# A hybrid attention trunk on one core: a rewritten opening, VectorE a chunk ahead, and two pieces of work moved behind others

## The chip, the core and the metric

One core of a Trainium2 chip runs the whole program. The core has five engines with their own instruction queues: TensorE (PE; its weight loads are shown as PEld), VectorE (DVE), ScalarE (ACT), GpSimd (POOL) and SyncE (SP), which here only issues transfers. The metric is the device time of one launch in microseconds (us), the median over several runs; smaller is better.

## What is computed

Two layers over a sequence of 512 positions of width 1024 (`x`, kept transposed: 8 chunks of 128 features by 512 positions). Each layer normalises `x`, modulates it by a conditioning vector `c`, and multiplies the result `h` by one wide input matrix; two attention mixers (8 heads each) work on the parts, and an output matrix closes the layer.

```
c_act = silu(c)
for l in range(2):
    shift, scale, gate = split(c_act @ w_ada[l] + b_ada[l], 3)
    h = rms_norm(x, norm_g[l]) * (1 + scale) + shift
    fq, fk, fv, ff, fg, q_lat, kv_lat, k_r, mg = split(h @ w_in[l])
    y_fox = fox_attention(fq, fk, fv, log_sigmoid(ff + b_f[l])) * silu(fg)
    q = rms_norm(q_lat, q_norm_g[l]) @ w_uq[l];  q_rope = rope(q, cos, sin)
    kv = rms_norm(kv_lat, kv_norm_g[l]) @ w_ukv[l];  k_rope = rope(k_r, cos, sin)
    y_mla = mla_attention(q, q_rope, kv, k_rope) * silu(mg)
    x = x + gate * (concat(y_fox, y_mla) @ w_out[l])
return rms_norm(x, final_g)
```

Every large product of float32 numbers is made of three products of rounded operands: high by high, high by low, low by high, where the low part is what the rounding left (`mm3`, L238 to L241). So each weight tile and each chunk of `h` needs a cast on ScalarE (`hi_of`, L124) and a subtraction on VectorE (`lo_of`, L127).

## The kernel before

**The opening** is `start_first` (L417 to L507). SyncE loads `c`, spread over 128 partitions (512 KB, L145), then a 512 KB tile of the modulation matrix (`ada`), then the 8 chunks of `x` (256 KB each, L465), then `ada` and weights (`w_first`) in turns. ScalarE and VectorE make `cb`, twice the silu of `c` on all partitions. TensorE warms up on 20 dummy products (L473). ScalarE squares each chunk of `x` and TensorE adds the squares over partitions by a float32 product with ones (L477); `Ln` and `Exp` on ScalarE give `r`, the reciprocal root (L478, L479).

**The chunk loop** then takes the 8 chunks of features one after the other. For chunk k VectorE sums two `ada` tiles along the free axis (`along`, L271) into the scalars A and B (L457, L258), multiplies `x` by A and `r` (L385), ScalarE adds B and casts (`hh`, L388), VectorE makes the rest (`hl`, L389); the weights of the chunk are cast and split as above (L124, L127, a piece of 512 columns and one of 304). TensorE then runs 21 products for the chunk: three for a 48-column tile called small (the forget gates and the rotary key), three for the first key tile, three for the first query tile, and twelve for the four tiles of `v`. The eight chunks add into seven banks of PSUM. The angles for the rotary embedding (`trig`) are computed in the loop, between the chunks' own work.

**Behind the chunk loop** `mix` runs six steps in order (`before`): the forget gates with the rotary key (`small`, L546), the first query and key (L655, L673), the first gate, and the query and key of the second pair of heads. The first gate and that query and key are projections of 24 products each, whose weights come through three buffers for the high and three for the low part. Then a loop over 64 units runs the scores and transposes of both mixers; between the units it takes work from a list (`fill_a`, `fill_b`), in the order of the table `ORD_A`.

**The order on each engine.** TensorE's order is the order of the code (`manual_schedule`). VectorE, ScalarE and the others are ordered by a scheduler at build time, and each engine then works strictly in that order. An instruction that waits therefore holds up all that stands behind it on its engine. Transfers are issued by SyncE, in order, and an issue can wait for a buffer or for an earlier transfer.

Of the kernel before, what the change touches and what calls it, by code (L numbers as in the profile page):

```python
# [52 lines left out]
WARM = 20  # L53
TRIG_AT = (2,2,3,5,6,)
FIRST_ORDER = (2,1,0,)
PRIO = 200
ORD_A = ((0,1,2,3,4,5,6,10,7,8,9,11,12,13,15,14,16,17,),(0,1,2,3,5,6,4,7,8,9,10,11,12,13,14,15,16,17,),)
# [11 lines left out]
PIN_ROWS = (0,2,3,)  # L69
PE_ENGINE = mybir.EngineType.PE  # L70
FIRST_W = 816
FIRST = ((512, P), (640, P), (768, 48))
# [12 lines left out]
def trunk(ctx, tc, xT_in, pos, c_in, cols_in, w_first, w_proj, w_small, w_v, w_uq, w_ukv, w_out, ada_0, ada_r, out):  # L85
# [39 lines left out]

    def lo_of(dst, src, hi, eng=None):
        (eng or nc.vector).tensor_sub(out=dst, in0=src, in1=hi.bitcast(F32))  # L127
# [15 lines left out]
    for half in range(2):  # L143
        cs = slice(512 * half, 512 * half + 512)
        nc.sync.dma_start(out=cb[:, cs], in_=c_in[:, cs].broadcast_to([P, 512]))  # L145
        th = scr()
        nc.scalar.activation(out=th, in_=cb[:, cs], func=AF.Tanh, scale=0.5)
        nc.vector.scalar_tensor_tensor(out=cb[:, cs], in0=th, scalar=1.0, in1=cb[:, cs], op0=ALU.add, op1=ALU.mult)
# [38 lines left out]
    def trig():  # L187
# [5 lines left out]
        nc.vector.tensor_copy(out=ang, in_=pi)  # L193
        nc.vector.tensor_scalar(out=ang, in0=ang, scalar1=col(C_INV), scalar2=None, op0=ALU.mult)
        nc.vector.tensor_scalar(out=kk, in0=ang, scalar1=1.0 / TWO_PI, scalar2=ROUND_MAGIC,
                                op0=ALU.mult, op1=ALU.add)
        nc.vector.tensor_scalar(out=kk, in0=kk, scalar1=-ROUND_MAGIC, scalar2=None, op0=ALU.add)
        for part in (PI_A, PI_B, PI_C):
            nc.vector.scalar_tensor_tensor(out=ang, in0=kk, scalar=-part, in1=ang,
                                           op0=ALU.mult, op1=ALU.add)  # L200
        yield
        nc.scalar.activation(out=sin, in_=ang, func=AF.Sin)
        nc.scalar.activation(out=cos, in_=ang, func=AF.Sin, scale=0.5)
        yield
        nc.vector.tensor_mul(out=cos, in0=cos, in1=cos)
        nc.vector.tensor_scalar(out=cos, in0=cos, scalar1=-2.0, scalar2=1.0, op0=ALU.mult, op1=ALU.add)
# [21 lines left out]
    def parts_w(raw, n, eng=None):  # L228
        with prio(boost[0]):
            lo = wp.tile([P, 1024], F32R, tag="wl", bufs=W_BUFS, name=nm("wl"))  # L230
            hi = wp.tile([P, 1024], F32R, tag="wh", bufs=W_BUFS, name=nm("wh"))
            ins = hi_of(hi[:, :n], raw[:, :n])
            if hold[0] and "w" in PIN_S:
                behind(ins, hold[0], "after the forget gates")
            lo_of(lo[:, :n], raw[:, :n], hi[:, :n], eng)
# [33 lines left out]
    def along(raw, cs, dst):  # L269

        nc.vector.scalar_tensor_tensor(out=raw, in0=raw, scalar=0.5, in1=cb[:, cs], op0=ALU.mult, op1=ALU.mult,  # L271
                                       accum_out=dst)
# [95 lines left out]
    class Layer:  # L368
# [11 lines left out]
        def h_chunk(self, k, cs, x, r, lo_eng=None):  # L380
            l = self.l
            t = scr()
            b = B_c[l][:, k:k + 1]
            hh, hl = self.hh[k][:, cs], self.hl[k][:, cs]
            nc.vector.scalar_tensor_tensor(out=t[:, cs], in0=x[k][:, cs], scalar=A_c[l][:, k:k + 1], in1=r[:, cs],  # L385
                                           op0=ALU.mult, op1=ALU.mult)
            if lo_eng is None:
                nc.scalar.activation(out=hh, in_=t[:, cs], func=AF.Identity, bias=b)  # L388
                nc.vector.scalar_tensor_tensor(out=hl, in0=t[:, cs], scalar=b, in1=hh.bitcast(F32),  # L389
                                               op0=ALU.add, op1=ALU.subtract)  # L390
            else:
                nc.scalar.activation(out=t[:, cs], in_=t[:, cs], func=AF.Identity, bias=b)
                hi_of(hh, t[:, cs])
                lo_of(hl, t[:, cs], hh, lo_eng)
# [728 lines left out]
```

## Time and profile before

| | us |
|---|---|
| median of 3 runs | 581.97 |
| lowest, highest | 577.22, 582.1 |
| the profiled execution | 580.7 |
| its span, first to last instruction | 578.8 |
| TensorE busy in the span | 552.0 (95%) |
| VectorE busy | 435.2 (75%) |
| ScalarE busy | 369.7 (64%) |
| mean granted TensorE clock | 0.985 |

Times below count from the start of the span of the profiled execution. "Granted clock" is TensorE's clock as a share of full speed; in this profile it stands at 1.00 or at 0.50 (2.4 and 1.2 GHz). A 512-column product of rounded operands starts 0.23 us after the one before it at full clock and 0.43 us after it at half clock. An idle time in brackets at the end of a row is what the engine waited before that instruction, and for whom.

### The profile page before, as it was taken

The numbers are of one execution on the slowest core, as the hardware profiler recorded it, in microseconds if no ns is written. First come the engines' busy times: TensorE is split into PE (matmuls) and PEld (weight loads), VectorE is DVE, ScalarE is ACT, GpSimd is POOL, SyncE is SP. The second block draws the span as 40 slices with busy tenths as digits, with TensorE's granted clock in tenths as the row PEclk, the third lists the DMA queues.
The fourth block names the chain that finished last, engine by engine and source line by source line (L and its number), as shares of the span: only waits on it lengthen the run. The fifth ranks groups of instructions, "written<-read, shape, count | busy, mean of one in ns | idle before, by whom it ended". The sixth has DMA issues, their size and how long they took to land.

```text
span 578.8 us, 8543 instructions
## 1 busy us (share of the span) xinstructions
PE 552.0 (95%) x2932; PEld 438.7 (76%) x2932; DVE 435.2 (75%) x938; ACT 369.7 (64%) x787; POOL 32.7 (6%) x57
## 2 busy tenths in 40 slices
PE   8799989999899998999989999999999999999994
PEld 6477868777677676877988888877777767777893
DVE  2898777777758878969699486676597988964664
ACT  6343836766657878973377354667477777877642
POOL 4000020110001000000000030001001000000011
PEclk9799989999989999999999999999999999999998
DMA  8985134342313544769744324322133341441534
GB/s 283 404 315 168 51 114 147 112 147 74 112 47 79 170 130 129 226 236 303 249 142 145 110 78 147 110 75 75 56 110 87 93 116 46 134 128 36 170 104 145
DMA packets 36859, 81.08 MB, mean 140 GB/s; under 512 B 7616, under 2 KB 13760, under 8 KB 36816
## 3 DMA queue, kind: packets, MB, share of 16 engines
q1 hardware_dynamic: 35792, 80.28, 42.8%
q8 instruction: 23, 0.38, 0.3%
q0 software_dynamic: 1024, 0.27, 0.3%
q14 instruction: 20, 0.16, 0.1%
HBM read 72.36 MB, written 4.72 MB: 133 GB/s over the span
## 4 chain that ended last, share of the span: by engine, by line
PE 68%; DVE 13%; ACT 7%; DMA 7%; issue 3%; SPq 0%; POOL 0%; DVEq 0%; ACTq 0%; POOLq 0%
PE psp L239 13%; PE psp L241 13%; PE psp L240 13%; PE psa L625 5%; PE pst L613 4%; PE pss L239 3%; DMA scr<-mrow 3%; PE pss L241 3%; PE pss L240 3%; DVE wl L127 2%; DMA raw<-in_w_out 2%; PE pss L693 2%; ACT wh L124 1%; ACT p L601 1%; DVE st L599 1%
## 5 line engine op out<-in xcount | busy, mean ns | idle before, releaser
L239 PE MATMUL psp<-sl,wh 128*128 128x512 f32 (+1 forms) x488 | 188.7, 387 | 0.1
L241 PE MATMUL psp<-sl,wl 128*128 128x512 f32 (+1 forms) x488 | 179.7, 368 | 3.7 <-DVE wl L127 3.7
L240 PE MATMUL psp<-sl,wh 128*128 128x512 f32 (+1 forms) x488 | 178.9, 367 | 0.0
L241 PEld LDWEIGHTS psp<-sl,wl 128*128 128x128 f32 x488 | 92.9, 190 | 20.2 <-DVE wl L127 4.8
L239 PEld LDWEIGHTS psp<-sl,wh 128*128 128x128 f32 x488 | 93.5, 192 | 12.6 <-ACT vf L411 0.4
L240 PEld LDWEIGHTS psp<-sl,wh 128*128 128x128 f32 x488 | 93.6, 192 | 11.1 <-DVE sl L127 0.2
L127 DVE TENSOR_TENSOR wl<-raw,wh 128x1024 fp32r<-128x1024 f32 (+1 forms) x62 | 73.4, 1186 | 26.1 <-ACT wh L124 25.6
L601 ACT ACTIVATE p<-pss,st 128x128 f32<-128x128 f32 (+3 forms) x128 | 67.3, 527 | 25.8 <-DVE st L599 25.2
L124 ACT CAST wh<-raw 128x1024 fp32r<-128x1024 f32 (+1 forms) x63 | 63.5, 1013 | 30.0 <-DMA raw<-in_w_out 9.4
L604 ACT ACTIVATE p<-p,st 128x128 f32<-128x128 f32 (+3 forms) x128 | 70.9, 564 | 17.1 <-DVE st L602 16.7
L599 DVE TENSOR_REDUCE st<-pss 128x1 f32<-128x128 f32 (+3 forms) x128 | 61.8, 484 | 21.8 <-PE pss L695 14.9
L613 PE MATMUL pst<-ident,p 128*128 128x128 f32 x320 | 57.0, 276 | 0.2 <-ACT p L604 0.2
L619 ACT COPY pT<-pst 128x512 f32<-128x512 f32 (+2 forms) x72 | 31.6, 439 | 24.7 <-PE pst L613 24.0
L124 ACT CAST sl<-scr 112x512 fp32r<-112x512 f32 (+1 forms) x48 | 29.4, 616 | 19.5 <-DVE scr L631 15.4
L613 PEld LDWEIGHTS pst<-ident,p 128*128 128x128 f32 x320 | 37.9, 142 | 4.1 <-ACT p L604 0.8
L127 DVE TENSOR_TENSOR sl<-scr,sl 112x512 fp32r<-112x512 f32 (+1 forms) x48 | 32.7, 685 | 5.8 <-ACT sl L124 5.4
L602 DVE RECIPROCAL st<-st 128x1 f32<-128x1 f32 x128 | 19.7, 157 | 19.9 <-ACT p L601 19.1
L271 DVE SCALAR_TENSOR_TENSOR adr<-adr,cb 128x1024 f32<-128x1024 f32 x24 | 29.1, 1214 | 3.8 <-DMA adr<-in_ada_r 3.7
L639 POOL DMA_DIRECT2D sl<-csq x16 | 9.2, 574 | 327.6 <-issue 157.6
L239 PE MATMUL pss<-sl,sl 112*128 112x256 f32 (+2 forms) x64 | 23.0, 359 | 3.5 <-ACT p L601 3.2
L617 DVE COPY pT<-pst 128x384 f32<-128x384 f32 (+2 forms) x56 | 25.2, 451 | 0.4 <-PE pst L613 0.2
L388 ACT ACTIVATE sl<-scr,B 128x256 fp32r<-128x256 f32 (+1 forms) x24 | 12.8, 574 | 19.7 <-DVE scr L385 17.3
(195 smaller groups left out, 894.4 us busy)
## 6 DMA issues: line engine op xcount, KB each, us to landing
raw<-in_w_proj SPq DMA_DIRECT2D x36, 512.0 KB, 3.5
adr<-in_ada_r SPq DMA_DIRECT2D x24, 512.0 KB, 3.5
raw<-in_w_out SPq DMA_DIRECT2D x20, 512.0 KB, 4.3
sl<-in_w_v SPq DMA_DIRECT2D x16, 256.0 KB, 5.0
sl<-in_ada_r SPq DMA_DIRECT2D x16, 256.0 KB, 5.0
vm<-in_ada SPq DMA_DIRECT2D x6, 512.0 KB, 6.0
pT<-in_ada SPq DMA_DIRECT2D x6, 512.0 KB, 6.7
sl<-in_xT SPq DMA_DIRECT2D x8, 256.0 KB, 6.1
```

Source lines behind the costliest of these rows:

```text
L124: return nc.scalar.copy(out=dst, in_=src) if scale == 1.0 else nc.scalar.mul(out=dst, in_=src, mul=scale)
L127: (eng or nc.vector).tensor_sub(out=dst, in0=src, in1=hi.bitcast(F32))
L239: nc.tensor.matmul(out=ps, lhsT=lh, rhs=rh, start=first, stop=False)
L240: nc.tensor.matmul(out=ps, lhsT=lh, rhs=rl, start=False, stop=False)
L241: nc.tensor.matmul(out=ps, lhsT=ll, rhs=rh, start=False, stop=last)
L271: nc.vector.scalar_tensor_tensor(out=raw, in0=raw, scalar=0.5, in1=cb[:, cs], op0=ALU.mult, op1=ALU.mult, accum_out=dst)
L599: nc.vector.tensor_reduce(out=st[:, 0:1], in_=s[:, :w], op=ALU.max, axis=AX, negate=True)
L601: nc.scalar.activation(out=p[:, :w], in_=s[:, :w], func=AF.Exp, bias=st[:, 0:1], accum_out=st[:, 1:2])
L604: nc.scalar.mul(out=p[:, :w], in_=p[:, :w], mul=st[:, 2:3])
L613: nc.tensor.transpose(out=tp[:, j * P:(j + 1) * P], in_=p[:, j * P:(j + 1) * P], identity=ident)
L619: nc.scalar.copy(out=dst, in_=src)
L625: nc.tensor.matmul(out=ps[64 * a:64 * a + 64, j * P:T], lhsT=v[:, j, 64 * heads[a]:64 * heads[a] + 64], rhs=pTs[a][:, PT_J * j + P * j:PT_ ...
```

## The change

- **Opening.** `c` is loaded as one row of 4 KB and activated on one partition; two products with a row of ones spread it over the partitions, and ScalarE copies them to `cb`. The positions are loaded third, the first five chunks of `x` next, then the first `ada` tile and the rest of `x`. The angles are computed before the chunk loop. Chunks 1, 3 and 5 of `x` are squared on VectorE and added there to the square of the chunk before, so TensorE gets five products with squares and not eight. There are 12 dummy products at first, 5 after the spreading products, and 3 of 512 columns behind the last product with squares. The table of the logarithm is loaded between the squares of chunks 6 and 7, and none is loaded for the forget gates later.
- **Chunk loop.** VectorE's and ScalarE's orders are now pinned (`queue`), from strings of letters: m for a modulation step, h for a step of `h`, w for a step of the weights, capitals for the next chunk. The products of a chunk are ordered by turn: all seven tiles with high weights and `hh`, then with `hl`, then six with low weights. The small tile is 112 columns wide and carries its low weights beside the high ones, so it takes two products: 20 for a chunk.
- **Rotary key.** Its four VectorE instructions leave `small` and become a piece of fill (`key`, number 18 in `ORD_A`), behind the first latent projection, in both layers.
- **Second gate moved behind.** In the first layer's list, gate 8 now stands behind the third key 11 and the sums 9.

```diff
-WARM = 20
-TRIG_AT = (2,2,3,5,6,)
-ORD_A = ((0,1,2,3,4,5,6,10,7,8,9,11,12,13,15,14,16,17,),(0,1,2,3,5,6,4,7,8,...
+WARM, WARM_1, WARM_2 = 12, 5, 3
+SQ_V, CB_AT, ANGLES = (1, 3, 5), (2, 4), 2
+TRIG_AT = (3, 4)
+ORD_A = ((0,18,1,2,3,4,5,6,10,7,11,9,8,12,13,15,14,16,17,),(0,18,1,2,3,5,6,4,7,8,...
+LOGS_AT = 6
+FIRST_W, FIRST_S, FIRST = 832, 768, (512, 640)
...
+    def queue(engine, ins):
+        if engine in line:
+            if line[engine]:
+                behind(ins, line[engine], "order of the first chunks")
+            line[engine] = ins.ins.name
+        return ins
...
-        nc.sync.dma_start(out=cb[:, cs], in_=c_in[:, cs].broadcast_to([P, 512]))
+    nc.sync.dma_start(out=c_row[0:1, :], in_=c_in)
+    nc.scalar.activation(out=c_act[0:1, :], in_=c_row[0:1, :], func=AF.Tanh, scale=0.5)
...
             def split_first(k):
+                queue("a", hi_of(hi[:, 512:FIRST_W], b[:, :FIRST_W - 512]))
+                yield
+                queue("a", hi_of(hi[:, :512], a))
+                yield
+                queue("v", lo_of(lo[:, 512:FIRST_S], b[:, :FIRST_S - 512], hi[:, 512:FIRST_S]))
+                queue("v", lo_of(hi[:, FIRST_S + SM_H:FIRST_S + SM_ALL], b[:, FIRST_S - 512:FIRST_S - 512 + SM],
+                                 hi[:, FIRST_S:FIRST_S + SM]))
+                yield
+                queue("v", lo_of(lo[:, :512], a, hi[:, :512]))
+                yield
...
             for k in range(KC):
                 sq = scr()
-                nc.scalar.activation(out=sq, in_=x0[k], func=AF.Square)
-                nc.tensor.matmul(out=total, lhsT=ones, rhs=sq, start=k == 0, stop=k == KC - 1)
+                if k in SQ_V:
+                    queue("v", nc.vector.tensor_mul(out=sq, in0=x0[k], in1=x0[k]))
+                    queue("v", nc.vector.tensor_add(out=sq, in0=before, in1=sq))
+                else:
+                    queue("a", nc.scalar.activation(out=sq, in_=x0[k], func=AF.Square))
...
+                if k == LOGS_AT:
+                    queue("a", nc.scalar.preload_act_table_set("natural_log_exp_and_others"))
...
+            for _ in range(WARM_2):
+                nc.tensor.matmul(out=first[0], lhsT=ones, rhs=x0[0], start=True, stop=True)
+            make(0, "mmwwhhwhwWMHM")
...
+                    make(k + 1, "hwwMhwWHM")
...
+                for turn, (ws, hs) in enumerate(((hi, self.hh), (hi, self.hl), (lo, self.hh))):
...
+        def key(self):
+            yield 0.0
+            t = self.key_in
             u, v = scr(), scr()
             nc.vector.tensor_mul(out=u[:SM, :], in0=t[:SM, :], in1=cosT[:SM, :])
```

Three places in the built programs show what the prediction speaks of. **ScalarE at the end of the opening**, from the last squares (`scr<-sl`) through `Ln` and `Exp` (`aux`) and the casts of the first weights (`wh`) to the first chunk of `h`. Before:

```order
L476 ACTIVATE scr_230<-sl_87 128x512
L476 ACTIVATE scr_233<-sl_88 128x512
L478 ACTIVATE aux_167<-pst_163,eps_c 128x512
L124 CAST wh_246<-sl_180 128x512
L479 ACTIVATE aux_167<-aux_167 128x512
L124 CAST wh_246<-sl_181 128x304
L388 ACTIVATE sl_146<-scr_255,B_125 128x512
```

And now:

```order
L519 ACTIVATE scr_240<-sl_87 128x512
L530 ACT_TABLE_LOAD
L519 ACTIVATE scr_244<-sl_88 128x512
L532 ACTIVATE aux_247<-pst_160,eps_c 128x512
L533 ACTIVATE aux_247<-aux_247 128x512
L124 CAST wh_265<-sl_186 128x320
L124 CAST wh_265<-sl_185 128x512
L399 ACTIVATE sl_143<-scr_268,B_122 128x512
```

A table load now stands between the last two squares, and both casts stand between `Exp` and the first chunk of `h`.

**VectorE in one round of the chunk loop** (`sums` are the `along` sums, `A` and `B` the scalars, `scr` is `x` by A by `r`, `sl` with `B` is `hl`, `wl` the low weights). Before:

```order
L258 TENSOR_TENSOR B_125<-sums_168,cols 128x1
L385 SCALAR_TENSOR_TENSOR scr_277<-sl_82,A_123,aux_167 128x512
L271 SCALAR_TENSOR_TENSOR raw_259,sums_168<-raw_259,cb 128x1024
L389 SCALAR_TENSOR_TENSOR sl_155<-scr_277,B_125,sl_147 128x512
L457 TENSOR_SCALAR A_123<-sums_168,b_109,cols 128x1
L271 SCALAR_TENSOR_TENSOR raw_261,sums_168<-raw_261,cb 128x1024
L127 TENSOR_TENSOR wl_308<-sl_263,wh_309 128x512
L127 TENSOR_TENSOR wl_308<-sl_264,wh_309 128x304
```

And now:

```order
L477 TENSOR_TENSOR B_122<-sums_164,cols 128x1
L137 TENSOR_TENSOR wl_300<-sl_289,wh_301 128x256
L137 TENSOR_TENSOR wh_301<-sl_289,wh_301 128x48
L282 SCALAR_TENSOR_TENSOR vm_161,sums_164<-vm_161,cb 128x1024
L473 TENSOR_SCALAR A_120<-sums_164,b_106,cols 128x1
L401 SCALAR_TENSOR_TENSOR sl_153<-scr_303,B_122,sl_145 128x512
L137 TENSOR_TENSOR wl_300<-sl_288,wh_301 128x512
L396 SCALAR_TENSOR_TENSOR scr_344<-sl_84,A_120,aux_247 128x512
L282 SCALAR_TENSOR_TENSOR pT_162,sums_164<-pT_162,cb 128x1024
```

The same work stands in a round, with one instruction more (the 304 columns are now 256 and 48), and the next chunk's `along` and product with `x` stand between this chunk's steps.

**VectorE behind the chunk loop**, from the forget gates' scan (`scr` from two `scr`) on; `csk` and `csq` are its results, `wl` from `raw` the low weights of the projections, `mrow` the rotary key, `gate` the first gate. Before, behind the scan:

```order
L580 TENSOR_TENSOR scr_603<-lat_581,cosT 48x512
L576 CAST csk<-scr_592 32x512
L576 CAST csq<-scr_592 32x512
L577 TENSOR_TENSOR csk<-scr_592,csk 32x512
L577 TENSOR_TENSOR csq<-scr_592,csq 32x512
L581 TENSOR_TENSOR scr_604<-lat_581,sinT 48x512
L662 SCALAR_TENSOR_TENSOR sl_614<-psp_242,sl_614 64x512
L582 TENSOR_TENSOR mrow<-scr_603,scr_604 16x512
L583 TENSOR_TENSOR mrow<-scr_603,scr_604 16x512
L664 CAST sl_615<-sl_614 64x512
L590 SCALAR_TENSOR_TENSOR gate_672<-scr_670,psp_645 128x512
L127 TENSOR_TENSOR wl_676<-raw_674,wh_677 128x1024
```

And now, from the row of the same low weights on:

```order
L137 TENSOR_TENSOR wl_674<-raw_672,wh_675 128x1024
L631 SCALAR_TENSOR_TENSOR scr_596<-scr_594,scr_595 32x512
L726 SCALAR_TENSOR_TENSOR sl_612<-psp_254,sl_612 64x512
L635 CAST csk<-scr_596 32x512
L635 CAST csq<-scr_596 32x512
L636 TENSOR_TENSOR csk<-scr_596,csk 32x512
L636 TENSOR_TENSOR csq<-scr_596,csq 32x512
L728 CAST sl_613<-sl_612 64x512
L137 TENSOR_TENSOR wl_760<-raw_758,wh_761 128x1024
L654 SCALAR_TENSOR_TENSOR gate_670<-scr_668,psp_643 128x512
L644 TENSOR_TENSOR scr_823<-lat_584,cosT 48x512
```

The low weights of the third projection (the second pair's key) moved from behind the scan, the key and the gate to ahead of the scan, and the rotary key moved behind the gate.

## Rows read from the trace of the kernel before

**Rows 1.** Page, part 1: busy time of each engine and its share of the span.
```profile
PE 552.0 (95%) x2932; PEld 438.7 (76%) x2932; DVE 435.2 (75%) x938; ACT 369.7 (64%) x787; POOL 32.7 (6%) x57
```

**Rows 2.** Windows: stretch, length, busy time per engine (instructions), granted clock, DMA share, GB/s.
```profile
0.00:19.58 19.58, 13.87 (x56) 9.50 (x56) 7.46 (x18) 11.69 (x18) 6.05 (x17) 0.99 0.89 314
19.58:27.88 8.30, 7.52 (x22) 5.36 (x23) 8.30 (x18) 2.44 (x5) 0.00 (x0) 0.62 1.04 407
27.88:32.71 4.83, 4.83 (x22) 3.75 (x21) 4.83 (x11) 1.58 (x3) 0.00 (x0) 1.00 1.04 400
73.40:83.00 9.60, 6.85 (x23) 5.39 (x23) 7.37 (x10) 1.98 (x3) 2.95 (x6) 0.82 0.36 115
156.80:163.20 6.40, 4.42 (x21) 3.74 (x20) 5.50 (x11) 3.08 (x7) 0.00 (x0) 0.73 0.24 83
```

**Rows 3.** Chain that ended last, opening: start, us, engine or transfer and line.
```profile
2.20 0.43 SPq L439
2.67 5.64 DMA sl<-in_xT
8.34 0.64 ACT scr L476
9.02 7.15 PE pst L477 x16
```

**Rows 4.** Timeline, ScalarE in the opening: start, us, line, operation, [idle before].
```profile
7.02 1.28 ACT L462 ACT_TABLE_LOAD   x1
...
16.19 0.69 ACT L478 ACTIVATE aux<-pst,eps_c 128x512 f32<-128x512 f32 x1 [2.10 <-PE pst L477]
16.78 0.61 ACT L124 CAST wh<-sl 128x512 fp32r<-128x512 f32 x1
17.29 0.63 ACT L479 ACTIVATE aux<-aux 128x512 f32<-128x512 f32 x1
17.82 0.43 ACT L124 CAST wh<-sl 128x304 fp32r<-128x304 f32 x1
```

**Rows 5.** Page, part 6: transfers, count, KB each, median us from issue to landing.
```profile
sl<-in_xT SPq DMA_DIRECT2D x8, 256.0 KB, 6.1
...
cols<-in_cols SPq DMA_DIRECT2D x1, 40.5 KB, 1.9
```

**Rows 6.** Timeline, VectorE through one round of the chunk loop.
```profile
25.74 0.27 DVE L457 TENSOR_SCALAR A<-sums,b,cols 128x1 f32<-128x1 f32 x1
25.92 1.22 DVE L271 SCALAR_TENSOR_TENSOR raw<-raw,cb 128x1024 f32<-128x1024 f32 x1
...
27.07 1.07 DVE L127 TENSOR_TENSOR wl<-sl,wh 128x512 fp32r<-128x512 f32 x2
28.05 0.15 DVE L258 TENSOR_TENSOR B<-sums,cols 128x1 f32<-128x1 f32 x1
28.12 0.75 DVE L385 SCALAR_TENSOR_TENSOR scr<-sl,A,aux 128x512 f32<-128x512 f32 x1
...
30.59 0.27 DVE L457 TENSOR_SCALAR A<-sums,b,cols 128x1 f32<-128x1 f32 x1
```

**Rows 7.** Timeline behind the chunk loop, ScalarE, VectorE and TensorE.
```profile
59.91 1.27 ACT L411 COPY vf<-pss 128x512 f32<-128x512 f32 x2
...
61.91 0.50 PE L239 MATMUL psp<-sl,wh 128*128 128x512 f32 x1
...
67.09 1.21 DVE L572 TENSOR_TENSOR_SCAN scr<-scr,scr 32x512 f32<-32x512 f32 x1 [2.81 <-ACT scr L569]
...
76.31 0.51 PE L241 MATMUL psp<-sl,wl 128*128 128x512 f32 x1 [2.75 <-DVE wl L127]
```

**Rows 8.** Timelines, TensorE's first score of all and two later waits.
```profile
83.04 0.28 PE L693 MATMUL pss<-sl,sl 128*128 128x256 f32 x1
...
158.82 0.43 PE L693 MATMUL pss<-sl,sl 128*128 128x256 f32 x1 [1.98 <-DVE sl L682]
...
219.03 0.44 PE L239 MATMUL pss<-sl,sl 112*128 112x384 f32 x1 [1.58 <-ACT p L601]
```

More of the change, by code (lines that the diff above doesn't have):

```diff
@@ new lines, in modulate, with make @@
+                yield
+                queue("v", along(ada[0, k], ALL1, d[:, 0, s]))
+                queue("v", nc.vector.tensor_add(out=B_c[0][:, s], in0=d[:, 0, s], in1=cols[:, C_BA + k:C_BA + k + 1]))
+                yield
+            steps = {}
+            def make(k, order):
+                for i, c in ((k, "mhw"), (k + 1, "MHW")):
+                    for name, g in zip(c, (modulate, lambda k: self.h_chunk(k, ALL, x0, r), split_first)):
+                        if i < KC and (i, name.lower()) not in steps:
+                            steps[i, name.lower()] = g(i)
+                for c in order:
+                    i = k if c in "mhw" else k + 1
+                    if i < KC:
+                        next(steps[i, c.lower()])
@@ L464, in start_first @@
+            for _ in range(ANGLES):
+                next(angles)
             for k in range(KC):
                 nc.sync.dma_start(out=x0[k], in_=xT_in[:, k, :])
+                if k == 4:
+                    load_ada(1, 0)
             load_ada(0, 0)
@@ L470, in start_first @@
             load_first(1)
-            next(angles)
             for _ in range(WARM):
+                nc.tensor.matmul(out=total[:, 0:P], lhsT=ones, rhs=ones, start=True, stop=True)
+            spread_c = [bank("p") for _ in range(2)]
+            for half in range(2):
+                nc.tensor.matmul(out=spread_c[half], lhsT=ones[0:1, :], rhs=c_act[0:1, 512 * half:512 * half + 512],
+                                 start=True, stop=True)
+            for _ in range(WARM_1):
                 nc.tensor.matmul(out=total[:, 0:P], lhsT=ones, rhs=ones, start=True, stop=True)
@@ L496, in start_first @@
                 hi, lo = w[k]
[L497 to L501 removed]
+                for turn, (ws, hs) in enumerate(((hi, self.hh), (hi, self.hl), (lo, self.hh))):
+                    a, b = turn == 0 and k == 0, turn == 2 and k == KC - 1
+                    if turn < 2:
+                        nc.tensor.matmul(out=first[2][:SM_ALL, :], lhsT=hi[:, FIRST_S:FIRST_S + SM_ALL], rhs=hs[k],
+                                         start=a, stop=turn == 1 and k == KC - 1)
+                    for j in (1, 0):
+                        o = FIRST[j]
+                        nc.tensor.matmul(out=first[j], lhsT=ws[:, o:o + P], rhs=hs[k], start=a, stop=b)
+                    for ti, ps in vps.items():
+                        nc.tensor.matmul(out=ps, lhsT=hs[k][:, ti * P:(ti + 1) * P], rhs=ws[:, :512], start=a, stop=b)
             for _ in range(TRIG_AT.count(KC)):
@@ L1025, in enter_second @@
         for k in range(KC):
-            lay[1].h_chunk(k, cs, lay[0].x, r)
+            for _ in lay[1].h_chunk(k, cs, lay[0].x, r):
+                pass
         if half == 1:
```

116 lines of the change are left out of this document (53 added, 63 removed).

## Prediction

> **What bounds the kernel now.** I read the busy times first: TensorE is busy for 552.0 of 578.8 us [rows 1], so only places where it waits or runs slowly can give time. The windows by stage show them [rows 2]: it is fully busy at full clock in most stretches, but not before 19.58 (the opening), not in the first chunk (8.30 us where the next takes 4.83, granted clock 0.62), not at 73.40 to 83.00 (clock 0.82) and not at 156.80 to 163.20 (clock 0.73). Last I read what ended each wait. In the opening the chain runs through the loading of `x`, the squares and eight products of 0.89 us each [rows 3], then `Ln`, `Exp` and the casts on ScalarE [rows 4]. At 76.31 a projection had waited 2.75 us for low weights from VectorE, which had itself waited 2.81 us for ScalarE's logarithm ahead of the scan [rows 7]. At 158.82 a score had waited 1.98 us for the third key's low part [rows 8]. The change touches all four places. Behind them both kernels run the same TensorE work, so I carry a gain there to the end.
>
> **Start of the first chunk.** The fourth issue stood at 2.20 [rows 3]; `x` now takes that place. Between its issue and landing 1.9 us (41 KB) is the low bound and 6.1, `x`'s own median behind a megabyte of other loads, the high one [rows 5]. Only small loads stand ahead, so I take 3.5, nearer the low end: chunk 0 at 5.7 (bounds 4.1 and 8.3). Chunk 6 comes eight pieces of 256 KB later (six chunks and one `ada` tile), at 400 GB/s [rows 2] 0.66 us each: 11.0. Then, each behind the other on ScalarE [rows 3, 4]: square 0.64, table load 1.28, square of chunk 7 0.64, one product 0.89, `Ln` 0.69, `Exp` 0.63; with 0.1 between engines that is 15.9. Now both casts stand ahead of the first `hh`: 0.43 and 0.61; `hh` itself is like `Ln`, 0.7. The first product starts at 17.7 instead of 19.58: 1.9 us earlier (bounds 16.1 to 20.3, so a loss of 0.7 is possible). Spreading `c` by two products and two copies, the angles (ten VectorE instructions on 64 columns) and their table load fill time in which these engines now wait for `x`; uncovered, each table load would cost its 1.28. The three squares moved to VectorE take three products of 0.89 off TensorE, which then no longer ends this chain.
>
> The Trainium skill, "ScalarE: Activation LUTs", section "Rules for kernel authors", tells to budget about 2.7 us for every switch to a different table set. Here the load takes 1.28 us and the next square starts at its end [rows 3, 4]; by the page's budget the first product would come 1.4 us later, and the sum would be 571 and not 570.
>
> **The first chunk.** The three dummies of 0.89 end at 17.2, so TensorE idles for about 0.5 us before the first product, where it had idled 3.4 (16.17 to 19.58 [rows 2, 3]); I expect full clock. With low parts needed only in the second and third turn, TensorE's 20 products take 4.6 us (21 take 4.83 [rows 2]). But the second chunk waits for VectorE. From the first `hh` on it does [rows 6] `hl` 0.7, low weights 0.6, `along` 1.15, A 0.2, `x` by A 0.7, `along` 1.15, B 0.15, and ScalarE the second `hh` 0.7; with waits of 0.1 that makes 5.45 against 8.30: 2.85 us gained.
>
> **The other chunks.** Here nothing is gained. A round of VectorE took 4.85 us [rows 6], just the 4.83 of TensorE [rows 2]. It now holds the same work with one instruction more, about 0.06: 4.91, above TensorE's 4.6. VectorE sets the pace, TensorE idles 0.3 a chunk, and six rounds lose 0.45 us; the last chunk's products, one fewer, give 0.1 back. Its loads need 1.47 MB a round, 3.7 us at 400 GB/s, and stay hidden. The loop ends 4.4 us earlier, at 57.4 instead of 61.76.
>
> **Behind the loop.** The first gate needs a bank that a copy of `v` frees. Before, `v` ended tile by tile; now all four end within the last 0.7 us, and ScalarE does the key's cast and three copies first, 0.63 each [rows 7]. TensorE then waits 1.3 us and starts the gate at 58.65 instead of 61.91 [rows 7]: 3.2 us are left. The third projection's low weights now stand ahead of the scan. Their buffer is free at 57.4, their cast comes behind five more ScalarE instructions, at about 61.2, and VectorE ends them near 63, long before the 69.6 at which that projection starts. The wait of 2.75 us goes, and with it the half clock behind it. From the gate's start to the first score took 21.1 us [rows 7, 8]; 72 products at 0.23 are 16.5. First score at 75.2 instead of 83.04: 7.8 us. The key's four instructions hide behind the scores: its result is needed only by the second mixer, and TensorE waits for VectorE nowhere near it.
>
> **Second gate.** The third key is made one projection, 24 products or 5.5 us, earlier, so the 1.98 us wait goes, and the half clock behind it: 6.40 us at a mean clock of 0.73 with 1.98 idle [rows 2, 8] make up 3.7 us with what the slow products cost. The gate needs less behind its products than the key did. Bounds: 0, if the sums' root, now computed between the key's instructions on VectorE, is as late as the key was; 3.7. I take 3.0, since the root needs few and small instructions.
>
> **Sum.** 580.7 is the profiled execution. 1.9 + 2.85 - 0.45 + 0.1 - 1.2 + 4.6 + 3.0 = 10.8, which gives **569.9, so 570**. The median of the runs shown is 1.3 above that execution and the lowest 3.5 below it, and I widen the range by that.
>
> **Rivals.**
> - *The second wait stays* (the root or a bank ends it as late as the key did): 572.9. For it: VectorE is busy 5.50 of the 6.40 us there [rows 2]. Against: the instruction waited for is the key's.
> - *The start does not move*, since the loads bound it: chunk 0 would start at 19.6, 571.8. For it: 1.04 of the DMA engines' time is taken in the first chunk [rows 2]. Against: the 512 KB of spread `c` are gone from ahead of `x`.
> - *The clock falls at the new wait of 1.3 us* ahead of the first gate. It fell behind waits of 2.75 and 1.98 us, not behind 1.58 at 219.03 [rows 8] nor 1.2 in the opening. Half clock then cost about 1.8 us: 571.7.
> - *The wait behind the loop stays*, with the low weights late for another reason (their load, the cast in a longer ScalarE queue): 4.6 less, 574.5. Against it: 6 us of slack.
> - *Slower*: VectorE's pace leaves TensorE idle 0.3 us in every chunk, and the clock might answer such gaps by staying at half. A chunk would take 20 times 0.43, 8.5 us, 3.6 above VectorE's pace; eight chunks cost 29 us, 599. It decides from the third such chunk on, where 10.9 us are lost. Against it: at half clock TensorE would have no gaps, and from such a stretch it rose to full clock within the first chunk [rows 2].
>
> Of this last one the Trainium skill speaks in "TensorE: Matmul & The Clock Gate", section "A second HAM failure mode: psum-queue depth-cycling": frequent short idle times between groups of products can make the clock swing between its levels. In this trace no idle time of 1.6 us or less lowered it.
>
> **How the numbers follow.** Chances: forecast 0.58, second wait stays 0.13, start does not move 0.11, clock falls once 0.08, wait behind the loop stays 0.05, slower 0.03; two of the small ones together 0.02. The forecast's own range, from the bounds of the start (16.1 to 20.3), of the second gate and of the runs, is 566 to 574; with the next cases the range is 565.5 to 576. What a measurement of this kernel can tell from no change is about 1%, 5.8 us: faster means below 576.2. That holds in every case but the slower one and joint ones: 0.92 faster, 0.05 within, 0.03 slower.
>
> **What would show it.** Right: first chunk's products near 17.7 at clock 1.00; chunk starts 4.9 apart with VectorE without idle time and TensorE with 0.3 each; first gate about 1.3 us behind the loop's end, waiting for ScalarE's copy of `v`; no wait for low weights ahead of the first score, which stands near 75; no wait of a score on a key's cast near 150. Wrong: a half clock in the chunk loop, chunk starts farther apart than 5 us, or a new wait of over 2 us between 60 and 160.

## The result

The changed kernel takes 572.5 us (median of 4 runs, 571.5 to 573.6) against 580.9 for the kernel before beside it: a ratio of 0.985, interval 0.982 to 0.989. Timed a second time, beside three of the experiments, it took 574.4 (8 runs) against 580.7, a ratio of 0.990 (0.987 to 0.994). So it is faster by 1 to 1.5%, some 6 to 8 us. The forecast was 570.0 with a range of 565.5 to 576.0, and "faster". The profiled execution took 571.8 us, 8.9 less than that of before; 10.8 had been forecast.

The page's first part shows TensorE still at its limit, with 2.9 us less work than in [rows 1]; VectorE has 8 us more.

```profile
PE 549.1 (96%) x2922; PEld 433.9 (76%) x2922; DVE 443.3 (78%) x951; ACT 366.1 (64%) x784; POOL 33.0 (6%) x57
```

Windows of the changed kernel (columns as in [rows 2]): the opening, the first chunk, one round of the loop, the last chunk, and the place of the third key.

```profile
6.00:13.00 7.00, 6.84 (x19) 3.13 (x18) 6.08 (x14) 5.21 (x10) 1.01 (x2) 0.76 1.03 362
19.07:24.86 5.79, 4.84 (x20) 3.65 (x20) 5.61 (x12) 1.13 (x3) 0.00 (x0) 1.00 1.03 397
29.70:34.91 5.21, 5.08 (x21) 3.57 (x20) 5.14 (x12) 1.63 (x4) 0.00 (x0) 1.00 1.03 296
56.05:60.70 4.65, 4.65 (x20) 3.65 (x20) 4.54 (x6) 3.87 (x6) 0.00 (x0) 1.00 0.23 32
150.00:157.00 7.00, 4.68 (x33) 3.84 (x31) 6.10 (x18) 4.20 (x9) 0.00 (x0) 1.00 0.53 151
```

The first chunk now runs at full clock (0.62 in [rows 2]), but lasts 5.79 us and not 4.65 like the last one, where TensorE is never idle; VectorE is busy for 5.61 of the 5.79. The same holds for every round: 5.21 us, with VectorE busy for 5.14. The opening, which had full clock before, now has half clock in the middle (0.76).

The chain that ended last, in the opening of the changed kernel (answers [rows 3]):

```profile
9.67 2.01 PE pst L523 x2
11.70 0.70 DVE scr L516
12.50 0.70 DVE scr L517
13.25 2.86 PE pst L523 x6
16.13 0.70 ACT aux L532
```

The product of the first pair takes 2.01 us, at half clock; VectorE waits for the scratch tile that it frees (11.70); the third pair is added at 12.50, and behind it stand three products in a row until 16.1.

Timelines behind the loop (answer [rows 7, 8]): TensorE's first gate, VectorE's low weights and scan, the first score of all, the third key's place and the wait near 212.

```profile
61.85 0.50 PE L250 MATMUL psp<-sl,wh 128*128 128x512 f32 x1 [0.98 <-ACT vf L420]
...
65.29 1.21 DVE L137 TENSOR_TENSOR wl<-raw,wh 128x1024 fp32r<-128x1024 f32 x1
66.42 1.20 DVE L631 TENSOR_TENSOR_SCAN scr<-scr,scr 32x512 f32<-32x512 f32 x1
...
78.33 0.28 PE L757 MATMUL pss<-sl,sl 128*128 128x256 f32 x1
...
153.25 1.13 PE L372 MATMUL pst<-ident,scr 128*128 128x128 f32 x8 [2.31 <-DVE scr L363]
...
211.74 0.45 PE L250 MATMUL pss<-sl,sl 112*128 112x384 f32 x1 [0.43 <-ACT p L665]
```

The wait of 2.75 us ahead of the first score is gone, and the score stands at 78.33 instead of 83.04. At the second gate there is a new wait of 2.31 us, for the latent's root on VectorE.

Where the time went, from the starts of the same instruction in both profiles (gain so far): first product 0.5, second chunk 3.0, end of the loop 1.1, first gate **0.1**, first score 4.7, behind the second gate (the score at 156.5) 6.3, at 349 us 7.6, end 8.8. In this profile all that the opening won was gone again at the first gate.

### The profile page after: what moved, and what is told of

The parts are those of the page before. It is cut to its first block, busy times and chain, and to the rows that moved or that the text cites. A ratio compares the mean times of both kernels' runs of the same rounds, so it can differ in the third digit from the quotient of the medians.

```text
span 570.0 us, 8541 instructions
## 1 busy us (share of the span) xinstructions
PE 549.1 (96%) x2922; PEld 433.9 (76%) x2922; DVE 443.3 (78%) x951; ACT 366.1 (64%) x784; POOL 33.0 (6%) x57
## 4 chain that ended last, share of the span: by engine, by line
PE 67%; DVE 15%; ACT 7%; DMA 7%; issue 3%; DVEq 0%; SPq 0%; ACTq 0%
PE psp L250 13%; PE psp L252 13%; PE psp L251 13%; PE psa L689 5%; PE pst L677 4%; DVE wl L137 3%; PE pss L250 3%; DMA scr<-mrow 3%; PE pss L251 2%; PE pss L252 2%; DMA raw<-in_w_out 2%; DMA sl<-in_ada_r 2%; PE pss L757 2%; ACT wh L124 1%; ACT p L665 1%
## 5 line engine op out<-in xcount | busy, mean ns | idle before, releaser
L250 PE MATMUL psp<-sl,wh 128*128 128x512 f32 (+1 forms) x472 | 180.6, 383 | 1.1 <-ACT vf L420 1.0
L252 PE MATMUL psp<-sl,wl 128*128 128x512 f32 (+1 forms) x472 | 171.7, 364 | 1.4 <-DVE wl L137 1.4
L251 PE MATMUL psp<-sl,wh 128*128 128x512 f32 (+1 forms) x472 | 171.3, 363 | 0.0
L252 PEld LDWEIGHTS psp<-sl,wl 128*128 128x128 f32 x472 | 89.1, 189 | 16.5 <-DVE wl L137 2.0
L250 PEld LDWEIGHTS psp<-sl,wh 128*128 128x128 f32 x472 | 89.5, 190 | 11.7 <-ACT vf L420 1.4
L251 PEld LDWEIGHTS psp<-sl,wh 128*128 128x128 f32 x472 | 89.6, 190 | 10.2 <-DVE sl L137 0.3
L665 ACT ACTIVATION_READ_ACCUMULATOR p<-pss,st 128x1 f32 x128 | 25.3, 197 | 0.0
```

Source lines behind the costliest of these rows:

```text
L250: nc.tensor.matmul(out=ps, lhsT=lh, rhs=rh, start=first, stop=False)
L251: nc.tensor.matmul(out=ps, lhsT=lh, rhs=rl, start=False, stop=False)
L252: nc.tensor.matmul(out=ps, lhsT=ll, rhs=rh, start=False, stop=last)
L665: nc.scalar.activation(out=p[:, :w], in_=s[:, :w], func=AF.Exp, bias=st[:, 0:1], accum_out=st[:, 1:2])
```

## The experiments

All kernels compute the whole reference. The ratios are to the kernel before, in runs on the same chip; where less than 1% is at stake I compare starts of instructions in the profiles. A profile is one execution, and some lie well below the median of their kernel (rows128 571.7 against 574.5, apart 570.4 against 572.6).

**1. Only the two moves behind the loop.** The kernel before, with the key and the order of the changed one:

```diff
-            u, v = scr(), scr()          # in small()
+            self.key_in = t              # and a generator key(), 18 in fill_a
-ORD_A = ((0,1,2,3,4,5,6,10,7,8,9,11,12,...
+ORD_A = ((0,18,1,2,3,4,5,6,10,7,11,9,8,12,...
```

> The kernel before with only the two moves of work behind the chunk loop (rotary key apart from the forget gates, third key ahead of the second gate); its opening and its chunk loop stay as they were. Theory A, the opening and the loop give nothing that is left at the first gate (it starts at 61.85 us after the change and at 61.91 before it), and all of the gain comes from the two moves: first gate near 61.9, first score near 78.5 instead of 83.0, profiled time near 572. Rival B, the gain of the loop (1.1 us at its end) and of the opening is real and reaches the end in part: first gate later than 62.5 or the wait for low weights ahead of the first score still there, 574 to 577.

Ratio 0.994 (0.991 to 0.996), profiled 574.5. The first score and its mask product, in this kernel:

```profile
78.35 0.28 PE L699 MATMUL pss<-sl,sl 128*128 128x256 f32 x1
...
78.59 0.23 PE L701 MATMUL pss<-msk_f,identb 128*128 128x128 bf16 x1
```

In the changed kernel the mask product starts at 78.57. So in the profiles the moves alone bring all of the gain that is there at the first score. They do not bring the rest: this kernel falls 1.0 us behind between 84 and 107, and 1.6 more behind the wait of 2.32 us at 154, where the clock fell (as it did in a second profile of the changed kernel, experiment 5). Theory A holds up to the first score, not at the end. And the profiled execution was the fastest of ten: by the medians the two moves bring 2.5 us (576.5 against 579.0), where key_back, on the same chip and with the new opening and loop, brings 5.1 (573.9). The intervals of these two ratios overlap a little; what the new opening and loop give behind the first score stays open.

**2. The key back.** The changed kernel with the four instructions again in `small()`.

> The changed kernel with the rotary key's four VectorE instructions back behind the scan of the forget gates, all else as changed. Theory A: low weights of the projection ahead of the first score come late again, TensorE waits some 2.7 us near 76 us and runs behind the wait at half clock; first score near 83 instead of 78.3, profiled time 571.8 + 4.6 = 576.4. Rival B: the wait was ended by the opening's earlier buffers and casts and not by the key's move: no wait over 1 us there, 572.

Rival B: no such wait; the first score's mask again at 78.59; ratio 0.991 (0.987 to 0.994), profiled 574.1 (1.6 us of the difference to 571.8 arise behind the wait of 2.32 us at 153, where the clock fell). Either half of the change, then, takes the wait away without the other. VectorE in moves_only:

```profile
67.05 1.21 DVE L572 TENSOR_TENSOR_SCAN scr<-scr,scr 32x512 f32<-32x512 f32 x1 [2.81 <-ACT scr L569]
...
71.68 2.34 DVE L127 TENSOR_TENSOR wl<-raw,wh 128x1024 fp32r<-128x1024 f32 x2
```

Here the wait for ScalarE ahead of the scan is as before (2.81), but the low weights behind it start at 71.68 and not at 75.04, since the key's four instructions (2.7 us) and the gate's (0.6) are out of the way; TensorE wants them at 73.6. In key_back one more low-weights instruction stands ahead of the scan, as in the changed kernel:

```profile
65.28 1.21 DVE L137 TENSOR_TENSOR wl<-raw,wh 128x1024 fp32r<-128x1024 f32 x1
66.42 1.21 DVE L631 TENSOR_TENSOR_SCAN scr<-scr,scr 32x512 f32<-32x512 f32 x1
```

**3. Both back.** Is it the early angles that put it there, because two table loads then fall away behind the loop? key_back with the angles in the loop:

```diff
-SQ_V, CB_AT, ANGLES = (1, 3, 5), (2, 4), 2
-TRIG_AT = (3, 4)
+SQ_V, CB_AT, ANGLES = (1, 3, 5), (2, 4), 1
+TRIG_AT = (2, 2, 3, 5, 6)
-                if k < 2:
-                    next(angles)
```

> The kernel key_back with the angles, too, back at their old places (cast and sine in chunks 3 and 4 of the loop), so that ScalarE loads the sine's table inside the loop and needs two loads of 1.28 us again for the forget gates' exponential and logarithm. Theory A, each of the two edits alone is enough to take away the wait ahead of the first score (the kernels moves_only and key_back both had it at 78.6): with both undone the wait of over 2 us for low weights near 76 us is back with half clock behind it, first score 4 to 5 us later than the loop's end alone explains. Rival B, neither matters and the planner's other choices took the wait away: first score at 78.6 plus only what ten more small VectorE instructions cost in the loop (about 1.2).

Profiled 584.4, a single execution, so that there is no ratio. VectorE behind its loop:

```profile
66.98 1.21 DVE L137 TENSOR_TENSOR wl<-raw,wh 128x1024 fp32r<-128x1024 f32 x1
...
70.78 1.21 DVE L629 TENSOR_TENSOR_SCAN scr<-scr,scr 32x512 f32<-32x512 f32 x1 [1.34 <-ACT scr L626]
```

The wait is not back: first gate at 63.55, the score's mask at 80.27, 16.7 us behind it as in the changed kernel. Theory A falls, and rival B holds. The table loads are there again and VectorE waits 1.34 us ahead of the scan, but the low weights stand in front of it. With the key and the angles back, what is left to put them there is the rest of the rewritten opening and loop; which of its edits the scheduler answers to was not taken apart. The run shows by itself what late angles cost: the sine waits for VectorE's angles in the middle of the loop, TensorE idles 2.05 us at 42.1 with half clock behind it, and the loop ends 1.7 us later; at 90.1 a score waits 1.87 us, again with half clock.

**4. The second gate's order.**

```diff
-ORD_A = ((0,18,1,2,3,4,5,6,10,7,11,9,8,12,...   # changed kernel
+ORD_A = ((0,18,1,2,3,4,5,6,10,7,8,9,11,12,...   # gate_back
+ORD_A = ((0,18,1,2,3,4,5,6,7,10,9,11,8,12,...   # sums_early
```

> The changed kernel with the second gate again ahead of the third key, all else as changed. Theory A: a score waits about 2 us for the third key's low part near 154 us as before the change, with half clock behind it, and the wait of 2.31 us for the latent's root goes: together 1.4 us longer, 573.2. Rival B: the root's wait stays as well (two waits), 575. Rival C: with the key's wait at full clock the two orders cost the same, 571.8.

Ratio 0.990 (0.987 to 0.994), profiled 573.1.

```profile
154.04 0.35 PE L757 MATMUL pss<-sl,sl 128*128 128x256 f32 x1 [1.98 <-DVE sl L746]
```

The score waits 1.98 us for the key as before the change, the root's wait is gone, and at 160 us the kernel is 1.5 us behind the first profile of the changed one, as theory A had it. But see experiment 5: in a second profile the changed kernel is itself 1.8 us later there.

> The changed kernel with the third query put behind the second latent and the latent's sums ahead of the third key, so that 48 products stand between the sums and the spread of their root instead of 24. Theory A: the root is then ready and the wait of 2.31 us at 150.9 us goes, nothing else waits: 571.8 - 2.3 = 569.5. Rival B: the sums themselves then wait for the latent's squares on ScalarE, or a score for its key, by as much: 571.8 or more.

Ratio 0.983 (0.980 to 0.987), profiled 570.5. The wait of 2.31 us is gone and at 163 us the kernel is 2.4 us ahead. At 349 us 1.5 are left, and 1.2 at the end: a score near 210 now waits longer for ScalarE's exponential, 1.44 us instead of 0.43. The waits for them in all, from the table of waits (us, times, longest):

```profile
PE pss L250 <- ACT p L665: 2.5, 5, 1.4
```

So the root's wait is real and costs 2.4 us where it stands; against the first profile of the changed kernel, half of it is returned later.

**5. The same kernel again**, profiled a second time.

> The changed kernel as it is, profiled and timed a second time, beside the next three. Theory A: whether the clock falls behind the wait of 2.31 us at 150.9 us, and in the opening at 9 to 12 us, differs from execution to execution; a second profile may show half clock where the first showed 1.00 behind the wait (then some 1.5 us more, 573.3), with all instruction starts ahead of it within 0.1 us of the first. Rival B: the clock follows from the kernel alone; the second profile shows the granted clocks of the first, 571.8.

Ratio 0.990, profiled 572.7. Theory A. One window, 155 to 156 us, of the first and of the second profile:

```profile
155.00:156.00 1.00, 1.00 (x6) 0.80 (x5) 1.00 (x4) 0.81 (x2) 0.00 (x0) 1.00 0.51 205
```

```profile
155.00:156.00 1.00, 1.00 (x6) 0.90 (x5) 1.00 (x2) 0.55 (x1) 0.00 (x0) 0.50 0.67 274
```

The wait ahead of it is the same (2.31 and 2.32 us), the clock behind it is not: 2.4 GHz once, 1.2 GHz the other time, which costs 1.6 us (the mask product behind the wait starts at 154.45 and 154.72, the next one at 156.49 and 158.32). The starts ahead of the wait agree to 0.1 us up to the first score and to 0.3 at the wait. With half clock the changed order and gate_back's stand within 0.3 us of each other (161.84 and 161.54 for the mask after that). The second gate's move is thus worth 1.5 us or nothing.

**6. No dummy products.**

```diff
-WARM, WARM_1, WARM_2 = 12, 5, 3
+WARM, WARM_1, WARM_2 = 12, 5, 0
```

> The changed kernel without the three dummy products ahead of the first chunk; TensorE then idles about 3 us from 16.1 to 19.1. Theory A: the clock is at half in the first chunk as it was before the change (about 6 us of it), so its 20 products take some 7.4 us where VectorE needs 5.8; second chunk near 26.5 instead of 24.86, 573.4 at the end. Rival B: the clock does not fall (a wait of 2.31 us behind a busy stretch left it at 1.00 in the changed kernel), second chunk at 24.9, 571.8.

Ratio 0.989 (0.984 to 0.993), profiled 571.7. The clock falls as theory A says:

```profile
20.00:21.00 1.00, 1.00 (x3) 0.76 (x3) 1.00 (x2) 0.00 (x0) 0.00 (x0) 0.50 1.00 385
```

but the second chunk starts only 0.4 us later (25.30), and the third at 30.02, with the changed kernel at 30.05. TensorE's slow products lie beside VectorE's 5.8 us. The dummies give TensorE its clock, and the kernel nothing in this execution. Theory A's mechanism is there, but half clock lasted about half as long as it had assumed. The first chunk here, and that of moves_only, which has the old opening:

```profile
19.05:25.30 6.25, 6.25 (x21) 4.96 (x22) 6.08 (x12) 1.69 (x4) 0.00 (x0) 0.73 1.03 398
```

```profile
20.00:27.63 7.63, 6.62 (x22) 4.87 (x22) 7.63 (x17) 2.38 (x5) 0.00 (x0) 0.78 1.04 408
```

In moves_only TensorE waits 1.0 us for `hl` behind its first product; the new order has no such wait. At no better clock (0.73 and 0.78) the rewritten chunk takes 1.4 us less, so that more than half of the 2.5 us that the first chunk gained is the order of work and not the clock. What the dummies save when half clock lasts as long as in [rows 2] (0.62 over 8.30 us) is not shown.

**7. All rows in the spreading products.**

```diff
-lhsT=ones[0:1, :], rhs=c_act[0:1, 512 * half:512 * half + 512]
+lhsT=ones, rhs=c_act[:, 512 * half:512 * half + 512]     # c_act set to zero first
```

> The changed kernel with the two spreading products of c over all 128 rows (127 of them zeros, set by one VectorE instruction while it waits for the loads) instead of one row. Theory A: the granted clock fell to 0.50 at 9 to 12 us because TensorE did little work in the products of one row at 6 to 8 us; with all rows it stays at 1.00, the product of the first pair of squares takes 0.9 us instead of 2.0, the wait of VectorE for its scratch tile (0.40 us) goes, Ln starts 0.5 us earlier (15.6) and the first chunk near 18.5; 571.3 at the end. Rival B: the rows do not matter, the clock falls all the same, first chunk at 19.07, 571.8.

Ratio 0.990 (0.985 to 0.994), profiled 571.7. The same window of the changed kernel and of this one:

```profile
10.00:11.00 1.00, 1.00 (x2) 0.09 (x1) 0.90 (x2) 0.68 (x2) 0.00 (x0) 0.50 1.06 348
```

```profile
10.00:11.00 1.00, 0.61 (x2) 0.30 (x2) 0.97 (x4) 0.99 (x3) 0.00 (x0) 1.00 1.06 397
```

The clock stays up and VectorE's wait for the scratch tile is gone, but the first chunk starts at 19.37, not at 18.5: `c` came later, and VectorE's row of work ends at 13.5 instead of 13.2. Nor is the cause of that clock settled: with one row it fell in nine profiles and stayed at 1.00 in two (apart and squares below). In apart, with the third pair of squares on VectorE as in the changed kernel, the first chunk starts at 18.85, 0.2 us earlier, and that pair waits for its load:

```profile
11.45 0.69 DVE L519 TENSOR_TENSOR scr<-sl 128x512 f32<-128x512 f32 x1 [0.17 <-DMA sl<-in_xT]
```

So half clock in the opening costs about 0.2 us at the first chunk, and the loads stand right behind it.

**8. A behind other work.**

```diff
-make(k + 1, "hwwMhwWHM")
+make(k + 1, "hwwMhMwWHMWM")    # a step each for sum, A, sum, B
```

> The changed kernel with other VectorE work between each sum over c and the instruction that uses its result (hl between the first sum and A, the small low part between the second sum and B). Theory A: a round takes 5.21 us and not 4.91 because A and B, directly behind their sums, wait 0.12 and 0.11 us for the accumulator to be read: rounds of 4.98, six of them 1.4 us, the chain of the first chunk 0.2 to 0.3 us; loop end near 59.0 instead of 60.7, 570.1 at the end. Rival B: the instructions themselves are longer than forecast; rounds stay at 5.2 and the time at 571.8.

Ratio 0.988 (0.982 to 0.993), profiled 570.4. In the order that ran, only A has other work in front of it; B still stands directly behind its sum. Rounds take 5.06 us, 0.15 less, and the first gate comes 1.05 us earlier. So the row of dependent instructions is part of the price of a round. The changed kernel's VectorE:

```profile
34.82 1.22 DVE L282 SCALAR_TENSOR_TENSOR vm<-vm,cb 128x1024 f32<-128x1024 f32 x1
35.97 0.08 DVE L282 DVE_READ_ACCUMULATOR vm<-vm,cb 128x1 f32 x1
36.09 0.27 DVE L473 TENSOR_SCALAR A<-sums,b,cols 128x1 f32<-128x1 f32 x1
...
39.35 0.08 DVE L282 DVE_READ_ACCUMULATOR pT<-pT,cb 128x1 f32 x1
39.46 0.16 DVE L477 TENSOR_TENSOR B<-sums,cols 128x1 f32<-128x1 f32 x1
39.57 0.42 DVE L137 TENSOR_TENSOR wl<-sl,wh 128x256 fp32r<-128x256 f32 x1
```

From the read of the accumulator to A 0.12 us pass, to B 0.11; A starts 1.27 us behind the start of its sum. In [rows 6] the instruction behind a sum is one that doesn't need it, and starts 1.15 us behind the sum's start (25.92 to 27.07).

**9. A and B on ScalarE** (chunks 2 to 7).

```diff
+queue("a", nc.scalar.activation(out=A_c[0][:, s], in_=d[:, 1, s], func=AF.Identity,
+                                bias=gb1[:, s], scale=cols[:, C_NG + k:C_NG + k + 1]))
+queue("a", nc.scalar.activation(out=B_c[0][:, s], in_=d[:, 0, s], func=AF.Identity,
+                                bias=cols[:, C_BA + k:C_BA + k + 1]))
```

> The changed kernel with A and B of chunks 2 to 7 on ScalarE (one instruction each on 128 columns of one element, with A as sum times scale plus a product made once), which is busy 1.6 of 5.2 us of a round. Theory A: VectorE's round loses A, B and their two waits for the accumulator, 0.53 us: 4.68 instead of 5.21, TensorE without idle time; six rounds 3.2 us, loop end near 57.6, first gate near 58.8, 568.7. Rival B: A and B come later over two engines and VectorE or the first product of a chunk waits for them: rounds of 5.0 or more, 570.6 or more.

Ratio 0.985 (0.981 to 0.989), profiled 570.8. Theory A, to 0.2 us, as far as the first score: rounds of 4.67 us, first gate at 58.94, the score's mask at 75.67, 2.9 us ahead. Its 568.7 at the end did not come. One round on VectorE and ScalarE, and the first gate:

```profile
34.83 0.08 DVE L284 DVE_READ_ACCUMULATOR vm<-vm,cb 128x1 f32 x1
34.83 0.75 DVE L403 SCALAR_TENSOR_TENSOR sl<-scr,B,sl 128x512 fp32r<-128x512 f32 x1
...
37.90 0.42 DVE L137 TENSOR_TENSOR wl<-sl,wh 128x256 fp32r<-128x256 f32 x1
```

```profile
38.02 0.29 ACT L488 ACTIVATE B<-sums,cols 128x1 f32<-128x1 f32 x1 [2.34 <-DVE pT L284]
```

```profile
58.94 0.50 PE L252 MATMUL psp<-sl,wh 128*128 128x512 f32 x1 [0.98 <-ACT vf L422]
```

On VectorE the sums no longer have a reader behind them. So VectorE's round set the pace of the loop, and six rounds cost what its length exceeds TensorE's by. At the end 1.1 us of it were left against the first profile of the changed kernel (waits for the exponentials 3.4 us instead of 1.7), 1.9 against the second, and 2.9 between the medians of the two on this chip (571.5 and 574.4).

**10. Other squares.**

```diff
-SQ_V, CB_AT, ANGLES = (1, 3, 5), (2, 4), 2
-LOGS_AT = 6
+SQ_V, CB_AT, ANGLES = (1, 3), (2, 4), 2
+LOGS_AT = 7
```

> The changed kernel with the last pair of squares back on ScalarE, each with a product of its own, and the table load behind the square of chunk 7 instead of ahead of it. Theory A: what made the first chunk start at 19.07 instead of 17.7 is VectorE, which from 5.2 to 13.2 us has c, the angles and six pair instructions one behind the other, and the three products that follow its last pair back to back; with the last pair on ScalarE its four squares end near 13, the last product near 14.4, Ln starts there instead of at 16.1, first chunk near 17.4, loop end and first gate 1.7 us earlier, 570.1. Rival B: the half clock of 9 to 12 us makes the six products of 1.8 to 2 us each the chain: first chunk no earlier than 18.7, 571.5 or more. Rival C: the first chunk starts near 17.4 but the loads of chunks 1 and 2 set the pace behind it: loop end as before, 571.8.

Ratio 0.990 (0.985 to 0.994), profiled 574.6. The first chunk starts at 18.88, so rival B's time came, but not for its reason: the clock was 1.00 here. TensorE's products and ScalarE's last square:

```profile
11.34 4.56 PE L523 MATMUL pst<-scr,ones 128*128 128x512 f32 x10 [0.37 <-DVE scr L517]
```

```profile
13.11 0.63 ACT L519 ACTIVATE scr<-sl 128x512 f32<-128x512 f32 x1 [0.48 <-DMA sl<-in_xT]
```

Five products of 0.91 us stand in line behind VectorE's second pair, where three stood behind the third; they end at 15.9 instead of 16.1. And chunk 7 landed at 13.1, so that here nothing could have put `Ln` ahead of 14.7.

**11. Together:** squares, ab_act and sums_early.

> The edits of squares, ab_act and sums_early together. Theory A: they act in different places and add up: 1.7 + 3.2 + 1.2 (what sums_early left at the end) = 6.1, 565.7. Rival B: what is gained ahead of the first gate is taken back by waits behind it, for weights or for the soft maximum's exponentials, as 1.2 of the 2.4 us that sums_early gained at 150 us were: 568 or more.

Ratio 0.979 (0.975 to 0.983), 567.6 us median. It beats both kernels, and is 6.9 us below the changed kernel's median beside it (574.4). By medians the parts come to the same (squares nothing, ab_act 2.9, and for the wait that sums_early takes away 2.4 with 1.6 for the half clock that may stand behind it), but the profiles do not show that sum: this one, at 568.1, is only 3.7 us below the first of the changed kernel and 4.6 below the second. 565.7 was not reached. It counted 1.7 for squares, but here six products, some at half clock, ran to 16.6 and the first chunk started at 19.59. And rival B came in part: 4.9 us ahead of the first profile at 181 us, this one is 3.7 ahead at the end.

## Why the prediction was right, and where it was not

- **Start of the first product: wrong.** Forecast 1.9 us earlier, measured 0.5. The failed step is "three products of 0.89 off TensorE, which then no longer ends this chain". It still ends it: the last three products wait in order behind VectorE's third pair and run from 13.25 to 16.1. Loads were later too: chunk 6 was squared at 11.56, as it landed (forecast 11.0), and in squares chunk 7 landed at 13.1, not 0.66 behind chunk 6. `Ln` came at 16.13 instead of about 14.6. From there to the product took 2.94 us, 0.2 less than forecast; VectorE's `x` by A and the casts ended within 0.1 us of each other (18.26 and 18.35). The angles, counted as filling idle time, were part of VectorE's row of work from 5.2 to 13.2.
- **First chunk: size right, 2.5 of 2.85, the mechanism in part.** Full clock, and the second chunk waits for VectorE, which took 5.79 us instead of 5.45. But the step that credits the dummies with this gain fails: without them (no_dummies) 0.4 us is lost there and nothing one chunk later, and 1.4 of the 2.5 us come with the new order of work at no better a clock (no_dummies against moves_only).
- **Other chunks: mechanism right, size wrong.** VectorE sets the pace, TensorE idles and the clock stays. A round was forecast at 4.91 and took 5.21; six of them cost 2.2 us and not 0.45. Mis-sized were A and B, which the forecast let follow their sums at no cost: 0.12 and 0.11 us behind them (apart, ab_act), 0.23 of the 0.30. The low part in two pieces cost 0.08 where 0.06 was forecast (0.34 and 0.12 from start to start, 0.38 in one piece).
- **Behind the loop: right.** TensorE waits 0.98 us for the copy of `v` (forecast 1.3), at full clock. As the loop ended 3.3 us later than forecast, the first gate moved by 0.1 and not by 3.2 us.
- **The wait ahead of the first score: right, 4.65 of 4.6,** and by the mechanism named: the low weights stand ahead of the scan, with time to spare (ready at 66.5; the projection starts 48 products of 0.23 us behind the gate, near 72.9). Not foreseen was that the two moves alone, or the rest of the change without the key's move, would do the same.
- **Second gate: the lower bound's reason came true.** "The sums' root is as late as the key was": it is later, 2.31 us against 1.98. The profile gained 1.5 of the 3.0, and that only because the clock stayed up; in the second profile nothing was gained.
- **Rivals.** "The second wait stays" and "the start does not move" both came true in part (1.5 and 1.4 us). "The clock falls at the new wait of 1.3 us" did not come (1.00 from the first chunk to the first score), nor did the slower case: gaps of 0.1 to 0.3 us in each chunk left the clock at 1.00. In "TensorE: Matmul & The Clock Gate", section "A second HAM failure mode: psum-queue depth-cycling", the Trainium skill tells of a kernel in which frequent short idle times between groups of products made the clock swing; gaps of this size did not do so in any chunk loop here.
- **The prediction's own signs.** Two of its signs of being wrong came: chunk starts 5.2 us apart (over 5), and a new wait of over 2 us between 60 and 160 (2.31 at the second gate). The third, half clock in the chunk loop, did not.
- **So the time came out near 570 by luck.** The terms as measured add up to 0.5 + 2.5 - 2.2 + 0.2 - 1.0 + 4.7 + 1.5 = 6.2 us. The other 2.6 of the profiled 8.8 were in no term: shorter waits of scores for ScalarE's exponentials (1.58 us in [rows 8] became 0.43) and small ones between 440 and 470. Of these last, 0.5 to 0.8 us are gained in all the other profiles, whichever edits the kernel has, so they may belong to the one profile of the kernel before and not to the change. The waits for exponentials depend on how the work happens to meet: in sums_early, ab_act and the second profile of the changed kernel they are longer again (2.5, 3.4 and 2.2 us in all, against 1.7). The second measurement, 574.4 against 580.7, is nearer to the 6.2.

## What to carry to other kernels

When a change takes work off the engine that ends a stage, add up the next engine's whole round, instruction by instruction, start to start, and put a price on every reader that stands directly behind its producer: VectorE's rounds, 0.36 us longer than before, ate 2.2 of the 3.0 us that the opening and the first chunk had won. A wait can have two sufficient cures in one change; undo each alone and then both before crediting either. And one profile is one execution: a wait of 2 us may or may not pull the clock down behind it, so its price here lay between its length and its length plus 1.6 us, and a second profile of the same kernel helps to tell which of a difference's terms can be trusted.

## What was not expected of the hardware

- The same wait of 2.3 us left TensorE's clock at 2.4 GHz in one execution and was followed by 1.2 GHz in another execution of the same kernel. Of the ten profiles with this wait (2.3 us, for the root) five fell behind it (again, key_back, moves_only, both_back, squares) and five did not. What decides it stays open.
- The clock also fell, in nine of eleven profiles with one-row products in the opening, while TensorE executed without a break (0.50 at 10 to 11 us, busy 1.00). With all rows it did not fall in the one profile taken, although TensorE was busy for only 0.61 of that microsecond. That the rows matter is a suspicion, not a finding.
- VectorE's angles ran slowly beside GpSimd, which builds masks until 7.1 us:

```profile
6.48 0.61 POOL L191 TENSOR_SCALAR_AFFINE_SELECT mrow<-mrow 16x512 f32<-16x512 f32 x1
```

```profile
5.16 0.62 DVE L204 CAST gate<-gate 128x64 f32<-128x64 int32 x1
5.82 0.64 DVE L205 TENSOR_SCALAR gate<-gate,cols 128x64 f32<-128x64 f32 x1
6.50 0.64 DVE L206 TENSOR_SCALAR gate<-gate 128x64 f32<-128x64 f32 x1
7.17 0.20 DVE L208 TENSOR_SCALAR gate<-gate 128x64 f32<-128x64 f32 x1
```

The first three take about as long as the GpSimd instruction beside them (0.61), and the fourth 0.20 once that engine is done. So the three make VectorE's row in the opening some 1.3 us longer, an estimate from these rows. In rows128, where GpSimd works until 7.6 us, the two that started ahead of 7.1 took 0.62 and 0.64 and the next two 0.20 and 0.19. The Trainium skill says in "SBUF — State Buffer", section "SBUF: two separate sides", that the two engines share a pair of ports, which a GpSimd instruction or one of certain kinds on VectorE holds to its end while the other is blocked; the trace fits that. No kernel with the masks elsewhere was run, so what it would bring is not shown.
